# Eight lower parts of a weight stream by accumulating transfers, decay rows through DRAM, and small products at other places

## The chip, the cores and the metric

The kernel runs on one core of one Trainium2 chip, as one program. The metric is device time in microseconds (us). PE is the tensor engine, DVE the vector engine, ACT the scalar (activation) engine, POOL the general engine, SP the sync engine, whose queue issues most DMA loads. The time before is 1096.87 us, the median of 3 runs (1096.74 to 1097.33).

## The reference

A two-layer model on 256 tokens of width 1024, in float32. Each layer has three residual sub-layers, each with its own adaptive norm (`modulate`): a SwiGLU block, a mixer, a SwiGLU block. The mixer of the first layer is the hybrid, in which this change lies; that of the second is an mLSTM.

```python
def hybrid_mixer(h, w_in, w_out, ...):
    gate_lru, x_lru, z_ssd, xbc, dt_raw = jnp.split(h @ w_in, HYB_SPLITS, axis=-1)
    x_lru = causal_conv(x_lru, lru_conv_w, lru_conv_b)
    y_lru = rg_lru(x_lru, ...) * jax.nn.gelu(gate_lru)
    xbc = jax.nn.silu(causal_conv(xbc, ssd_conv_w, ssd_conv_b))
    ...
    dt = jax.nn.softplus(dt_raw + ssd_dt_bias)
    a = -jnp.exp(ssd_a_log)
    y = ssd_chunked(xs, dt, a, bm, cm) + ssd_d[:, None] * xs
    y = y.reshape(bsz, seq, SSD_WIDTH) * jax.nn.silu(z_ssd)
    y = rms_norm(y in 2 groups of 512, ssd_norm_g)
    return jnp.concatenate([y_lru, y], axis=-1) @ w_out
```

`ssd_chunked` works on two chunks of 128 tokens and 16 heads of 64. With `acs` the running sum of `dt * a` within a chunk, a head's weights between tokens are `exp(acs[t] - acs[s])` for s <= t, times the products of `C` and `B`; what the first chunk leaves for the second is weighted with `exp(acs[t])`. So every head needs its row `acs[t]` on all 128 partitions: the decay rows.

## The kernel before

**Weights.** All weights form one stream of 128x128 tiles in the order of use, in pieces of 8 tiles (128 x 1024 floats, 512 KB). `Weights._piece` loads a piece on SP's queue (`wraw`, 4 buffers), ACT writes its high part (`whi`, line 101, the value rounded to the format of the fast products), DVE the lower part, raw minus high (`wlo`, line 102). High and low buffers have three tags, taken in turn by `i % 3`, with two buffers each, so a piece takes the buffers of the piece six before it. `multiply` makes three products of each tile: high weight with high and with low activations, low weight with high activations (lines 443 to 445). A piece is 24 products. The stage of the hybrid starts at piece 66 (`starts[1]`) and has 54 pieces.

**Order.** A planner orders the instructions of each engine by the program's order and its own costs. Where that isn't wanted, the kernel adds edges: `W.behind(i, n, ins)` puts the high (n = 0) or low (n = 1) part of piece i behind an instruction; `stand(m, s, n)` puts a small product behind the n-th weight product of stage s; `in_one_go` keeps products together. `pump` starts the blocks of the adaptive norm (`ada`, 512 KB and one DVE operation over 128 x 1024 each) at the pieces of `ADA_PLAN`, behind the last lower part (`W.last`).

**The hybrid's order on PE.** `begin` makes the first four blocks (`bc`), then two blocks of `xbc`, the dt product, six more blocks of `xbc`, then a loop over c = 0..9 with the block `xl` of c and, two steps behind it, the blocks `z` and `ri` (LRU gates). In this loop stand the small products of the SSD part: `acs` (running sums, at c = 3), their transposition `acst` (at c = 4), the values and states of both groups. Then a loop over four pairs of blocks (m0 = 0, 2, 4, 6; four heads each): decay rows, `y` products, two gate blocks `gl`, and for m0 = 2 and 6 the group's norm. Then the projection out (`od`).

**The parts that the change touches.**
- dt: `dt_weights` keeps high and low parts of the dt weights in two tiles (`wdh`, `wdl`), and three products per k (lines 818 to 820) make 24.
- Decay rows: `decay_rows` writes the transposed sums as high and low part into `stk` (lines 864 and 865). For each pair four products with a selecting vector `sel` spread the rows over the partitions into PSUM (`ab`, line 974). ACT takes them from there: eight `Relu` with the bias `acs` (line 983), two `Exp` for `ce` (985), one `Exp` over all (986). DVE multiplies with `cb` and `C` (988, 992), then PE makes the 24 records of `y` (1008).
- Group norm: `rs_tokens` sums the squares of a group with four products, from the two halves of `gacc` (8 records of `rst_g`, line 359). Eight small DVE operations make the root (`rsy_g`, line 329), `spread` brings it to all partitions (`rsb_g`, line 405).
- The five scans of the LRU that stand around the second group's root are on line 1057.

## Time and profile before

| | |
|---|---|
| runs | 1096.74, 1096.87, 1097.33 us |
| profiled execution | 1097.25 us, its span 1095.5 us |
| busy, share of the span | PE 99%, weight loads 98%, DVE 84%, ACT 58%, POOL 1% |
| granted clock of PE | 0.999 of full speed |
| DMA | 272.34 MB, mean 249 GB/s |
| hybrid stage, first to last PE product | about 194 to 367 us |

Busy shares are means over the whole span; the stage in question is read by itself, in stretches. A PE product is shown from its start to its modelled end, and products overlap: the distance from start to start is what each costs. A row of a timeline has start, length, engine, line, operation, output and inputs, how many were merged, and in brackets the idle time ahead of it with what ended it. "Idle" there is shorter than the hole in the row of products, since the product before it is still running.

### The profile page before, as it was taken

The numbers are of one execution on the slowest core, as the hardware profiler recorded it, in microseconds if no ns is written. First come the engines' busy times: TensorE is split into PE (matmuls) and PEld (weight loads), VectorE is DVE, ScalarE is ACT, GpSimd is POOL, SyncE is SP. The second block draws the span as 40 slices with busy tenths as digits, with TensorE's granted clock in tenths as the row PEclk, the third lists the DMA queues.
The fourth block names the chain that finished last, engine by engine and source line by source line (L and its number), as shares of the span: only waits on it lengthen the run. The fifth ranks groups of instructions, "written<-read, shape, count | busy, mean of one in ns | idle before, by whom it ended". The sixth has DMA issues, their size and how long they took to land.

```text
span 1095.5 us, 23272 instructions
## 1 busy us (share of the span) xinstructions
PE 1083.8 (99%) x9315; PEld 1070.4 (98%) x9315; DVE 920.5 (84%) x1654; ACT 639.5 (58%) x1053; POOL 8.8 (1%) x28
## 2 busy tenths in 40 slices
PE   9999999999999999999999999999999999999997
PEld 7999999999999999999999999999999999999997
DVE  7999999899999899989698798979768868866552
ACT  5765555678986564554454455448776655544452
POOL 0000000000000000000000000010000000000000
PEclk9999999999999999999999999999999999999999
DMA  9889999556855489999848799963432664875551
GB/s 375 344 318 391 387 352 343 178 196 195 279 167 191 139 307 370 354 351 327 281 142 323 266 356 346 338 204 119 146 102 81 208 193 137 298 239 193 193 174 39
DMA packets 75534, 272.34 MB, mean 249 GB/s; under 512 B 8593, under 2 KB 9393, under 8 KB 75426
## 3 DMA queue, kind: packets, MB, share of 16 engines
q1 hardware_dynamic: 74592, 269.38, 69.7%
q8 instruction: 73, 1.20, 0.4%
q0 software_dynamic: 400, 1.04, 0.4%
q10 hardware_dynamic: 434, 0.43, 0.1%
q14 instruction: 35, 0.29, 0.1%
HBM read 269.77 MB, written 1.05 MB: 247 GB/s over the span
## 4 chain that ended last, share of the span: by engine, by line
PE 80%; DVE 12%; DMA 4%; issue 2%; ACT 1%; ACTq 0%; DVEq 0%; SPq 0%
PE gu L445 12%; PE gu L444 12%; PE gu L443 11%; PE od L445 10%; PE od L443 10%; PE od L444 10%; DVE wlo L102 4%; DMA wraw<-in_wst_dram 3%; PE zz L445 1%; PE zz L443 1%; PE zz L444 1%; DMA wgr<-in_ml_wg_dram 1%; DVE ada L262 1%; DVE xc L733 1%; PE gu_f L509 1%
## 5 line engine op out<-in xcount | busy, mean ns | idle before, releaser
L102 DVE TENSOR_TENSOR wlo<-wraw,whi 128x1024 fp32r<-128x1024 f32 x364 | 442.9, 1221 | 83.6 <-ACT whi L101 83.0
L101 ACT CAST whi<-wraw 128x1024 fp32r<-128x1024 f32 x364 | 378.2, 1050 | 210.9 <-DMA wraw<-in_wst_dram 80.2
L444 PE MATMUL gu<-hb,whi 128*128 128x256 f32 x1296 | 358.0, 276 | 0.4 <-DVE hb L668 0.3
L443 PE MATMUL gu<-hb,whi 128*128 128x256 f32 x1296 | 358.0, 276 | 0.0
L445 PE MATMUL gu<-hb,wlo 128*128 128x256 f32 x1296 | 357.9, 276 | 0.1
L444 PEld LDWEIGHTS gu<-hb,whi 128*128 128x128 f32 x1296 | 243.3, 188 | 0.8 <-DVE hb L668 0.8
L445 PEld LDWEIGHTS gu<-hb,wlo 128*128 128x128 f32 x1296 | 243.3, 188 | 0.2 <-DVE wlo L102 0.2
L443 PEld LDWEIGHTS gu<-hb,whi 128*128 128x128 f32 x1296 | 243.2, 188 | 0.0
L443 PE MATMUL od<-ph,whi 128*128 128x256 f32 x704 | 194.3, 276 | 0.0
L444 PE MATMUL od<-ph,whi 128*128 128x256 f32 x704 | 194.3, 276 | 0.0
L445 PE MATMUL od<-ph,wlo 128*128 128x256 f32 x704 | 194.3, 276 | 0.0
L262 DVE SCALAR_TENSOR_TENSOR ada<-ada,cact 128x1024 f32<-128x1024 f32 x144 | 175.3, 1218 | 1.4 <-DMA ada<-in_adaT_dram 1.3
L444 PEld LDWEIGHTS od<-ph,whi 128*128 128x128 f32 x704 | 132.1, 188 | 0.0
L445 PEld LDWEIGHTS od<-ph,wlo 128*128 128x128 f32 x704 | 132.1, 188 | 0.0
L443 PEld LDWEIGHTS od<-ph,whi 128*128 128x128 f32 x704 | 132.1, 188 | 0.0
L426 ACT CAST ph<-fg 128x256 fp32r<-128x256 f32 x88 | 35.1, 406 | 114.9 <-DVE fg L595 114.9
L427 DVE TENSOR_TENSOR ph<-fg,ph 128x256 fp32r<-128x256 f32 x88 | 36.4, 421 | 14.2 <-ACT ph L426 14.2
L416 ACT ACTIVATE sq_o<-x 128x256 f32<-128x256 f32 x42 | 17.5, 418 | 45.6 <-DVE x L571 40.6
L571 DVE SCALAR_TENSOR_TENSOR x<-od,gate,x 128x256 f32<-128x256 f32 x48 | 23.1, 481 | 24.4 <-PE od L445 24.2
L444 PE MATMUL zz<-hb,whi 128*128 128x256 f32 x128 | 36.2, 283 | 0.0
L445 PE MATMUL zz<-hb,wlo 128*128 128x256 f32 x128 | 36.1, 282 | 0.0
L443 PE MATMUL zz<-hb,whi 128*128 128x256 f32 x128 | 35.8, 279 | 0.0
(431 smaller groups left out, 1959.1 us busy)
## 6 DMA issues: line engine op xcount, KB each, us to landing
wraw<-in_wst_dram SPq DMA_DIRECT2D x366, 512.0 KB, 4.6
ada<-in_adaT_dram SPq DMA_DIRECT2D x144, 512.0 KB, 5.6
xn<-in_x_dram SPq DMA_DIRECT2D x2, 512.0 KB, 4.0
wgr<-in_ml_wg_dram POOLq DMA_DIRECT2D x3, 256.0 KB, 5.4
out_dram<-res SPq DMA_DIRECT2D x3, 128.0 KB, 2.4
out_dram<-res ACTq DMA_DIRECT2D x1, 256.0 KB
out_dram<-res SPq DMA_DIRECT2D x1, 256.0 KB, 2.9
cols<-in_cols_dram SPq DMA_DIRECT2D x1, 190.0 KB, 9.5
```

The source lines that it names most:

```text
L101: raw_hi = nc.scalar.copy(hi, raw)
L102: self.last = nc.vector.tensor_tensor(out=lo, in0=raw, in1=hi.bitcast(F32), op=ALU.subtract)
L262: return nc.vector.scalar_tensor_tensor(out=raw, in0=raw, scalar=1.0, in1=cact, op0=ALU.mult, op1=ALU.mult, accum_out=mods[s][:, m:m + 1])
L416: square = nc.scalar.activation(q, x, AF.Square).ins
L426: nc.scalar.copy(hi, src)
L427: nc.vector.tensor_tensor(out=both[:, 1, :], in0=src, in1=hi.bitcast(F32), op=ALU.subtract)
L443: m = nc.tensor.matmul(dst, wh, both[:, 0, :], start=start, stop=False, skip_group_check=True)
L444: W.products += [m, nc.tensor.matmul(dst, wh, both[:, 1, :], start=False, stop=False, skip_group_check=True), nc.tensor.matmul(dst, wl, bo ...
L445: nc.tensor.matmul(dst, wl, both[:, 0, :], start=False, stop=stop, skip_group_check=True)]
L509: W.products += [nc.tensor.matmul(dst, wh, rh, start=(k == 0), stop=False), nc.tensor.matmul(dst, wh, rl, start=False, stop=False), nc.ten ...
L571: nc.vector.scalar_tensor_tensor(out=xs_t[d], in0=dst, scalar=g[:, d:d + 1], in1=xs_t[d], op0=ALU.mult, op1=ALU.add)
L733: nc.vector.scalar_tensor_tensor(out=dst[:, o:], in0=src[:, :T - o], scalar=cw(j), in1=dst[:, o:], op0=ALU.mult, op1=ALU.add)
```

## The change

1. **Lower parts by accumulating transfers.** For the pieces 76, 79, 82, 85, 88, 91, 94 and 106 the lower part isn't made on DVE. ACT writes the negated value, rounded, into `wlo`, and a DMA on POOL's queue adds the piece from DRAM to it a second time. `W.last` stays at the last lower part made on DVE.
2. **Decay rows.** ACT copies the transposed sums into `rows`, SP stores them in DRAM (`kept`, 16 x 256), and `decay_tile` loads the rows of a pair's four heads on all partitions (`mt`, 512 KB, SP). The spreading products, `stk` and `sel` go. `decay_pair` then works in SBUF: one `Exp` for `ce` of both blocks, eight `Relu` and one `Exp` in place. The first two pairs' tiles are loaded at c = 5 and 7 and worked on at c = 7 and 9 of the loop before; those of the other two are loaded behind the `y` products of m0 = 0 and 2, whose buffers they take.
3. **Fewer products.** The dt weights lie with high and low side by side in one tile, so 16 products give both, and DVE adds the two results. DVE adds the two halves of `gacc` (`folded`) before the group's sum.
4. **Places.** `y` of m0 = 0 and 2 behind products 732 and 795 of the stage, the second group's sum behind 934 and its spread behind 995. The lower parts of the pieces 75 and 97 behind conv sums, of 105 and 109 behind the groups' roots. The scans behind the second root. The eight ada blocks of this stage over its pieces 22 to 34 rather than 37. The first group's outputs are split right behind its norm, within the loop over the pairs.

```diff
-SUMS = {"n1": (1, 11), "n2": (2, 11), "n4": (4, 14)}
+SUMS = {"n1": (1, 11), "n2": (2, 11), "n4": (4, 14), "g1": (1, 934)}
+SPREADS = {"n2": (2, 28), "g1": (1, 995)}
+ADDED = (76, 79, 82, 85, 88, 91, 94, 106)
...
-    (0, (17, 43), range(16, 40)), (0, (43, 65), range(48, 64)), (1, (22, 37), range(40, 48)),
+    (0, (17, 43), range(16, 40)), (0, (43, 65), range(48, 64)), (1, (22, 34), range(40, 48)),
...
             raw_hi = nc.scalar.copy(hi, raw)
-            self.last = nc.vector.tensor_tensor(out=lo, in0=raw, in1=hi.bitcast(F32), op=ALU.subtract)
...
+            if added:
+                low = nc.scalar.activation(lo, raw, AF.Copy, scale=-1.0)
+                nc.gpsimd.dma_start(lo, self.src[i].bitcast(F32R), accum_op=ALU.add)
+            else:
+                low = nc.vector.tensor_tensor(out=lo, in0=raw, in1=hi.bitcast(F32), op=ALU.subtract)
...
+                if i == 0:
+                    W.behind(starts[1] + 9, 1, taps[-1])
...
-            nc.tensor.matmul(b[:, 0:T], wdh, h[k][:, 0, :], start=(k == 0), stop=False)
-            nc.tensor.matmul(b[:, 0:T], wdh, h[k][:, 1, :], start=False, stop=False)
-            nc.tensor.matmul(b[:, 0:T], wdl, h[k][:, 0, :], start=False, stop=(k == ND - 1))
+            for i in range(2):
+                nc.tensor.matmul(b[:, 0:T], dt_parts[:, 32 * k:32 * k + P], h[k][:, i, :], start=(k == i == 0),
+                                 stop=(k == ND - 1 and i == 1))
...
+        nc.vector.tensor_tensor(out=dt, in0=both[:, :, 16:32], in1=dt, op=ALU.add)
...
-            nc.vector.tensor_copy(stk[0:16, :], b[0:16, 0:T])
-            nc.vector.tensor_tensor(out=stk[32:48, :], in0=b[0:16, 0:T], in1=stk[0:16, :].bitcast(F32),
-                                    op=ALU.subtract)
+            nc.scalar.copy(rows[0:16, :], b[0:16, 0:T])
+            nc.sync.dma_start(kept, rows[0:16, :])
+
+        def decay_tile(m0):
+            mt = wk.tile([P, 2, 2, 2, P], F32, tag="mt", name=f"mt{m0}", bufs=2)
+            nc.sync.dma_start(mt.rearrange("p n i c t -> p (n i c t)"),
+                                kept.rearrange("(q h) t -> q (h t)", q=4)[m0 // 2:m0 // 2 + 1].to_broadcast([P, 4 * T]))
+            decays[m0] = mt
...
+        def decay_pair(m0):
+            g = m0 // 4
+            mt = decays.pop(m0)
+            ce = wk.tile([P, 2, 2, P], F32, tag="ce", name=f"ce{m0}", bufs=2)
+            expo = nc.scalar.activation(ce.rearrange("p n i t -> p (n i) t"),
+                                        mt.rearrange("p n i c t -> p (n i) c t")[:, :, 1, :], AF.Exp)
+            for n in range(2):
+                for i in range(2):
+                    for c in range(2):
+                        hd = 2 * (m0 + n) + i
+                        nc.scalar.activation(mt[:, n, i, c, :], mt[:, n, i, c, :], AF.Relu,
+                                             bias=acs[:, c, hd:hd + 1], scale=-1.0)
+            nc.scalar.activation(mt, mt, AF.Exp, scale=-1.0)
...
+            return mt, ce, needed, expo
...
+                if c == 7:
+                    W.behind(starts[1] + 31, 1, taps[-1])
...
+            if c in (5, 7):
+                decay_tile(c - 5)
+            if c in (7, 9):
+                pairs[c - 7] = decay_pair(c - 7)
...
-            ab = [ax_bank(f"ab{m}") for m in pair]
...
-                    nc.tensor.matmul(b[:, i * T:(i + 1) * T], sel[:, hd:hd + 1].to_broadcast([P, P]), stk,
-                                     start=True, stop=True)
...
+            mt, ce, needed, expo = pairs.pop(m0) if m0 in pairs else decay_pair(m0)
...
+            if m0 < 4:
+                stand(products[0], 1, (732, 795)[m0 // 2])
...
+                folded = nc.vector.tensor_tensor(out=gacc[:, 0, :], in0=gacc[:, 0, :], in1=gacc[:, 1, :], op=ALU.add)
+            if m0 < 4:
+                decay_tile(m0 + 4)
...
-                roots.append(rs_tokens([gacc[:, 0, :], gacc[:, 1, :]], 512, f"g{g}", "q"))
+                roots.append(rs_tokens([gacc[:, 0, :]], 512, f"g{g}", "q"))
...
+                W.behind(starts[1] + (39, 43)[g], 1, rsqrt_ends[-1])
...
+                with tc.issue_after(second_root.ins):
+                    nc.vector.tensor_tensor_scan(out=xl[:, c, :], data0=av[:, c, :], data1=nq[:, c, :], initial=0.0,
+                                                 op0=ALU.mult, op1=ALU.add)
```

More of the change, by code (lines that the diff above doesn't have):

```diff
@@ L88, in __init__ @@
         self.splits = {}
+        self.last = None
         self.after = {}
@@ L99, in _piece @@
         hi, lo = (self.part_pool.tile([P, w], F32R, tag=f"{n}{'abc'[i % 3]}", name=f"{n}{i}") for n in ("whi", "wlo"))
+        added = i in ADDED
         with self.tc.high_priority(offset=self.ahead):
             raw_hi = nc.scalar.copy(hi, raw)
-            self.last = nc.vector.tensor_tensor(out=lo, in0=raw, in1=hi.bitcast(F32), op=ALU.subtract)
-        if i < 2:
-            self.tc.add_manual_dep(self.last.ins, self.first.ins.name, NOSYNC, reason="the first input first")
-        self.parts[i] = (hi, lo)
-        self.splits[i] = (raw_hi, self.last)
-        if i - 1 in self.splits:
-            for n in range(2):
-                self.tc.add_manual_dep(self.splits[i][n].ins, self.splits[i - 1][n].ins.name, NOSYNC, reason="in order")
+            if added:
[3 more added lines that the diff above has]
+                low = nc.vector.tensor_tensor(out=lo, in0=raw, in1=hi.bitcast(F32), op=ALU.subtract)
+        self.parts[i] = (hi, lo)
+        if self.splits:
+            self.tc.add_manual_dep(raw_hi.ins, self.splits[max(self.splits)][0].ins.name, NOSYNC, reason="in order")
+        if added:
+            self.splits[i] = (raw_hi, self.last)
+            return
+        if self.last is not None:
+            self.tc.add_manual_dep(low.ins, self.last.ins.name, NOSYNC, reason="in order")
+        self.last = low
+        self.splits[i] = (raw_hi, low)
         for n, ins in self.after.pop(i, ()):
@@ L144, in body @@
     partp = ctx.enter_context(tc.tile_pool(name="partp", bufs=2))
+    dramp = ctx.enter_context(tc.tile_pool(name="dramp", bufs=1, space=bass.MemoryType.DRAM))
     at = FIRST_PLACE
@@ L754, in exp_neg_abs @@
         return e, nc.scalar.activation(e, e, AF.Exp).ins
-    dt_parts = [cst.tile([P, 8 * 16 + 112], F32R, name=n) for n in ("wdh", "wdl")]
+    dt_parts = cst.tile([P, 480], F32R, name="wd")
     def dt_weights():
@@ L847, in hybrid @@
         acs = acs_wide[:, 0:32].rearrange("p (c h) -> p c h", c=2)
-        stk = sp.tile([P, T], F32R, name="stk")
-        nc.gpsimd.memset(stk.bitcast(F32), 0.0)
+        rows = sp.tile([P, T], F32, name="rows")
+        kept = dramp.tile([16, T], F32, name="kept")
         dec = sp.tile([P, 16], F32, name="dec")
@@ L872, in hybrid @@
         o = COL["lru_ba"]
-        sel = sp.tile([P, 16], F32R, name="sel")
+        sp.tile([P, 16], F32R, name="pad3")
         with tc.issue_after(W.normed.ins):
             nc.vector.tensor_scalar(out=hb, in0=cols[:, o:o + 16], scalar1=0.5, scalar2=None, op0=ALU.mult)
-            nc.vector.tensor_tensor(out=sel, in0=ident[:, 0:16], in1=ident[:, 32:48], op=ALU.add)
         b = ax_bank("bn", "p")
@@ L1028, in hybrid @@
             if m0 % 4 == 2:
-                roots.append(rs_tokens([gacc[:, 0, :], gacc[:, 1, :]], 512, f"g{g}", "q"))
+                roots.append(rs_tokens([gacc[:, 0, :]], 512, f"g{g}", "q"))
                 if g == 0:
                     group_norm(0)
-        ys = [sp.tile([P, 2, T], F32R, tag=f"ssd{m % 4}{m // 4}", name=f"ysb{m}") for m in range(8)]
-        for m in range(4):
-            split(xs[:, m, :], ys[m])
+                W.behind(starts[1] + (39, 43)[g], 1, rsqrt_ends[-1])
+                ys += [sp.tile([P, 2, T], F32R, tag=f"ssd{m}{g}", name=f"ysb{4 * g + m}") for m in range(4)]
+                if g == 0:
+                    for m in range(4):
+                        split(xs[:, m, :], ys[m])
+        second_root = rsqrt_ends[-1]
         yl, last = [], []
```

57 lines of the change are left out of this document (22 added, 35 removed).

## The prediction

> **What bounds the kernel now.** I read the page first (engine shares, the chain that ended last), then the waits of PE in the hybrid stage, then a table of stretches, then PE's order of time around each wait. From the page:
>
> ```profile
> PE 1083.8 (99%) x9315; PEld 1070.4 (98%) x9315; DVE 920.5 (84%) x1654; ACT 639.5 (58%) x1053; POOL 8.8 (1%) x28
> PE 80%; DVE 12%; DMA 4%; issue 2%; ACT 1%; ACTq 0%; DVEq 0%; SPq 0%
> ```
>
> PE is the bound: only fewer products or fewer holes between them shorten this kernel. The 12% of DVE in the chain say where the holes come from. The waits of PE between 212 and 332 us (total, times, longest):
>
> ```profile
> PE y L1008 <- DVE mt L988: 0.8, 1, 0.8
> PE z L443 <- DVE lru_x L733: 0.8, 1, 0.8
> PE rsb_g L405 <- DVE rsy_g L329: 0.7, 1, 0.7
> PE xbc L443 <- DVE ssd_x L733: 0.3, 1, 0.3
> ```
>
> Each is a wait for DVE. The stretches (busy us of PE, PEld, DVE, ACT, POOL, granted clock, DMA share, GB/s) say why:
>
> ```profile
> 220.00:250.00 30.00, 29.73 (x262) 29.56 (x261) 28.75 (x67) 23.07 (x42) 0.00 (x0) 1.00 0.57 186
> 250.00:283.00 33.00, 33.00 (x281) 31.96 (x279) 32.68 (x60) 26.90 (x52) 0.00 (x0) 1.00 0.67 222
> 283.00:296.00 13.00, 11.71 (x98) 11.18 (x96) 13.00 (x24) 12.74 (x31) 0.00 (x0) 1.00 0.89 297
> 296.00:332.00 36.00, 34.79 (x336) 33.32 (x337) 34.97 (x69) 31.68 (x64) 0.00 (x0) 1.00 0.51 167
> ```
>
> From 220 to 296 us DVE has 28.75 + 32.68 + 13.00 = 74.4 of 76 us of work, ACT 62.7. Both are near full here, at a granted clock of 1.00, so the stage has two engines a few per cent behind PE. The holes in order of time on PE (start, length, operation, idle before):
>
> ```profile
> 220.24 0.28 PE L445 MATMUL xbc<-hb,wlo 128*128 128x256 f32 x1
> 220.79 0.36 PE L443 MATMUL xbc<-hb,whi 128*128 128x256 f32 x1 [0.28 <-DVE ssd_x L733]
> ...
> 282.85 0.28 PE L445 MATMUL ri<-xlb,wlo 128*128 128x256 f32 x1
> 283.90 0.39 PE L443 MATMUL z<-hb,whi 128*128 128x256 f32 x1 [0.77 <-DVE lru_x L733]
> ...
> 295.28 0.28 PE L443 MATMUL gl<-hb,whi 128*128 128x256 f32 x1
> 296.41 0.33 PE L1008 MATMUL y<-mt,ssd 128*64 128x128 f32 x2 [0.85 <-DVE mt L988]
> ...
> 330.61 0.28 PE L445 MATMUL od<-ysb,wlo 128*128 128x256 f32 x1
> 331.61 0.46 PE L405 MATMUL rsb_g<-ident,rsy_g 128*128 128x128 f32 x2 [0.72 <-DVE rsy_g L329]
> ```
>
> A product takes 0.28 us, but the next starts 0.12 us after it (below). So a hole costs its start-to-start distance less 0.12: 0.43, 0.93, 1.01 and 0.88, together 3.25 us.
>
> **The change, part by part.**
>
> *Fewer dt products.* 24 products become 16. The first of them and the first product after them:
>
> ```profile
> 212.08 0.28 PE L818 MATMUL dtT<-hb,wdh 128*128 128x256 f32 x1
> ...
> 214.89 0.28 PE L443 MATMUL xbc<-hb,whi 128*128 128x256 f32 x1
> ```
>
> 2.81 us / 24 = 0.117 us each; 8 fewer are -0.94 us, all on PE. The added DVE sum over 128x32 elements costs PE nothing: DVE has it early, in a stage where its load falls (below).
>
> *Decay rows through DRAM, and fewer sum products.* From the chain in order of time, one pair's products, four spreads of decay rows and the eight sums of one group:
>
> ```profile
> 301.58 1.46 PE y L1008 x24
> 304.19 0.47 PE ab L974 x4
> 308.22 0.87 PE rst_g L359 x8
> ```
>
> The 16 `ab` products go: 16 x 0.117 = -1.87. Of the 16 records of `rst_g` eight go, because the two halves are added on DVE first: 8 x 0.109 = -0.87. In their place come one fold per group on DVE (256 elements per partition, about 0.4 us, a third of the lower part's 1.22 below) and DMAs on SP: one store and four 512 KB loads. PE work together: -0.94 - 1.87 - 0.87 = **-3.7 us**.
>
> *What queues behind the new DMAs.* SP issues in order. The tile loads for the third and fourth pair wait until PE has done with the buffers, and the weight loads behind them wait too. The high cast of the weight piece whose load comes next behind the third pair's tile load, and PE's first product with it:
>
> ```profile
> 288.15 1.04 ACT L101 CAST whi<-wraw 128x1024 fp32r<-128x1024 f32 x1
> ...
> 307.26 0.28 PE L443 MATMUL gl<-hb,whi 128*128 128x256 f32 x1
> ```
>
> There are 19 us between them. The loads (KB, median us to landing):
>
> ```profile
> wraw<-in_wst_dram SPq DMA_DIRECT2D x366, 512.0 KB, 4.6
> ```
>
> So this piece's load was issued by 283.5. Behind the tile load it waits for the end of `y0`, whose products start 46 products earlier than before: 296.41 less the hole of 1.01, less 46 x 0.115 = 5.3, less 0.47 for the `ab` products that stood between, is 289.6, and 291.1 with the 1.46 they take. Of the 19 us some 11 remain: nothing. If this cover were gone it would cost up to 7.6.
>
> *Eight lower parts.* One lower part on DVE, and two high casts on ACT:
>
> ```profile
> L102 DVE TENSOR_TENSOR wlo<-wraw,whi 128x1024 fp32r<-128x1024 f32 x364 | 442.9, 1221 | 83.6 <-ACT whi L101 83.0
> 217.54 2.01 ACT L101 CAST whi<-wraw 128x1024 fp32r<-128x1024 f32 x2
> ```
>
> DVE loses 8 x 1.22 = 9.8 us, ACT gains 8 x 1.0 = 8 us (the negated copy, same size as the cast), POOL gains eight issues. Seven of the eight lie between 217 and 283 us. DVE there: 74.4 - 7 x 1.22 = 65.9; two ada products that come earlier (1.2 each by size) and the second pair's multiplication (the 1.22 of the same size plus half) bring it to 70 of the some 73 us that the stretch then lasts. So three of the four holes, which are DVE lateness, lose their reason. ACT: 62.7 + 7 + 0.4 for the row copy, and the second pair's exponentials may come in from behind 296. Their first and last row, eleven instructions:
>
> ```profile
> 295.52 1.24 ACT L983 ACTIVATE mt<-ab,acs 128x128 f32<-128x128 f32 x4
> ...
> 298.09 1.19 ACT L986 ACTIVATE mt<-mt 128x1024 f32<-128x1024 f32 x1
> ```
>
> 3.8 us: ACT then has 73.9 in a stretch of 73. That is the price of this change, and I return to it.
>
> *The transfer's latency.* The trace has no accumulating transfer. The nearest rows besides that of the weight loads (a load by POOL; then the weight loads' min/median/max):
>
> ```profile
> wgr<-in_ml_wg_dram POOLq DMA_DIRECT2D x3, 256.0 KB, 5.4
> DMA to landing us min/median/max: 3.3/4.6/9.7
> ```
>
> Lower bound 3.3, the quickest load of this size. Upper bound 2 x 9.7 = 19.4: it reads both source and destination. I take 6.5, between the POOL row, which is the nearest in queue, and twice the SP median. Who waits: PE, for the lower part of that piece. The first such piece is the earliest and tightest. Its high cast starts at 217.54 (above); PE's first product of it:
>
> ```profile
> 226.33 0.28 PE L443 MATMUL xbc<-hb,whi 128*128 128x256 f32 x1
> ```
>
> After: 217.5 + 1.0 (cast) + 1.0 (copy) + 6.5 = 226.0. PE gets there 0.94 + 0.43 earlier, at 225.0: late by 1.0 us; since the cast may be issued a little sooner I take +0.7 (0 at 5.5 us or less, 13.9 at 19.4). A later one, the fifth:
>
> ```profile
> 248.63 1.04 ACT L101 CAST whi<-wraw 128x1024 fp32r<-128x1024 f32 x1
> ...
> 262.83 0.28 PE L443 MATMUL z<-hb,whi 128*128 128x256 f32 x1
> ```
>
> 14.2 us, less 2.0 and less 1.5 by which PE is earlier: 10.7 for the transfer. It is hidden at 6.5.
>
> The Trainium skill ("DMA: Bandwidth & Descriptors", section Anatomy of one DMA) fits a transfer from GpSimd as about 2.0 us plus bytes over 436 GB/s, an estimate of 3.2 us for 512 KB; by that the first piece is not late and the sum is 0.7 lower. The row of 4.6 us for the same size under this kernel's load disagrees with the fit already. The skill ("SBUF — State Buffer", section Summary: rules for kernel authors) also advises against a software-generated DMA under a busy DVE, since its descriptors starve while DVE runs in its two-port modes; by its section Who interferes with whom a two-input operation such as the lower part only takes a read port. By the advice alone the first piece would wait for one such operation more, by the other nothing; I add nothing.
>
> *Small products at other places.* Rows of DVE that made the holes: two lower parts ahead of the conv sums that `xbc` waits for; and the second group's root, from its first row to its last, with a scan before nearly each of its steps:
>
> ```profile
> 216.33 2.36 DVE L102 TENSOR_TENSOR wlo<-wraw,whi 128x1024 fp32r<-128x1024 f32 x2
> ...
> 324.43 0.16 DVE L373 TENSOR_SCALAR rsv_g<-rst_g 128x2 f32<-128x2 f32 x1
> ...
> 330.73 0.69 DVE L1057 TENSOR_TENSOR_SCAN lru_x<-lru_aq 128x256 f32<-128x256 f32 x1
> 331.33 0.14 DVE L329 SCALAR_TENSOR_TENSOR rsy_g<-rsw_g,rsy_g 128x2 f32<-128x2 f32 x1
> ```
>
> The root took 7 us for nine small steps; with the scans and a lower part behind it, it ends by about 326, and its spread is due at product 995 of the stage (it stood at 987), near 332: the last hole goes, -0.88. One of the two lower parts goes behind the conv sums: 1.2 us against a hole of 0.43, but PE comes 0.94 earlier for the dt products saved. Bounds -0.43 and +0.2; I take -0.3. The hole at 283 goes with DVE's load, -0.93. `y0` moves ahead from product 778 to 732, to 289.6 by the times of before (above). Its multiplications released PE at 296.41, so they have to come 7 us earlier. The rows they start from stood ready here before:
>
> ```profile
> 260.64 0.40 DVE L864 CAST stk<-acst 16x256 fp32r<-16x256 f32 x1
> ```
>
> From 260.6 the store and the tile load take two transfers, 9 us by the median above and 19 by the longest, then 4 us of exponentials and 2 of multiplications: 276 to 286, against 289.6 less the 2.8 that PE is then ahead, 286.8. It fits, without room at the upper end. If it does, the hole of 1.01 goes. Sum of the holes: -0.88 - 0.3 - 0.93 - 1.01 = **-3.1 us**. What is late next is ACT with its 73.9 in 73 us; I put +0.6 on it (0 if the second pair's exponentials stay behind 296, 3.1 if it brings all the holes back).
>
> *The sum.* -3.7 - 3.1 + 0.7 + 0.6 = **-5.5 us**. The profiled execution took 1097.25 us, 1.75 more than its span, 0.38 over the median of the runs: 1097.25 - 5.5 - 0.38 = **1091.4 us**. Before 212 and after 332 us I change nothing: PE is full there, so the end moves by what the stage gains.
>
> **The rivals.**
>
> 1. *ACT becomes the bound* (the waits change their engine). For it: 73.9 us of work in 73, its row of 12.74 in 13, `y0` due earlier. Against it: its high casts run 9 to 19 us ahead of PE and can give way. PE's work falls by 3.7, the holes stay as ACT's: 1096.87 - 3.7 = 1093.2, between 1092.5 and 1094.7.
> 2. *Slower: the accumulating transfers land too late.* Only PE waits for them, at the first piece. With every other gain kept (-3.7 - 3.1 + 0.6 = -6.2) it decides from a latency where the delay is 6.2: 5.5 + 6.2 = 11.7 us. At twice the longest load, 19.4, the first piece costs 13.9; the fifth one's 10.7 grows by the delay already taken and holds. Time 1096.87 - 6.2 + 13.9 = 1104.6; half way, at 15 us, 1100.2. For it: two reads for a write, a DMA share of 0.89 where the later pieces lie. Against it: 0.57 where the first lies, and POOL's median of 5.4.
> 3. *The change does nothing for the holes and the work saved turns into waits* (PE comes to each conv, root and pair earlier by what it saved, and DVE has only 3 us to spare in 73): 1096.9. Against it: the casts run 9 to 19 us ahead, so of 8.5 us less DVE work more than the 0.94 and 0.43 is left for the late operations.
> 4. *All of it works*: no late first piece and no ACT bound, 1096.87 - 3.7 - 3.25 = 1089.9, and down to 1088.8 if re-entries of PE after the removed insertions save 0.1 us each at some ten places.
>
> **How the numbers follow.** Forecast (1090.5 to 1092.5) 0.40; rival 4 (1088.8 to 1090.5) 0.20; rival 1 (1092.5 to 1094.7) 0.22; rival 3 (1094.7 to 1099.1) 0.06; rival 2 (above) 0.12. A measurement here tells 0.2% from nothing, 2.2 us: faster is 0.40 + 0.20 + 0.22 = 0.82, same 0.06, slower 0.12. The range leaves out rival 2 and the upper part of rival 3, 0.12 and some 0.04, and a little below rival 4: 1088.8 to 1096.0. The forecast's own range is 1090.5 to 1092.5.
>
> **What would show it.** Right: 16 `dtT` products and no `ab` on PE, eight `rst_g` records; no wait of PE for `lru_x`, `mt` or `rsy_g` between 212 and 332 us; the stretch from the stage's first dt product to the spread of the second group shorter by 5 to 6 us; DVE below full from 220 to 290. The transfers: their rows from issue to landing give the latency, 6.5 us or not; a PE wait at a lower part `wlo` for a DMA would show rival 2, and its length the price. ACT rows without a gap and PE waits for ACT would show rival 1. The prediction is wrong if new waits of PE add up to more than 3 us, or if the gain lies outside this stage.

## The result, and the profile after

Measured: **1108.4 us** (median of 4 runs, 1103.73 to 1111.23) against 1096.88 us before, a ratio of 1.0100 with a 95% interval of 1.0065 to 1.0135. The change makes the kernel slower; 1091.4 us was predicted. The profiled execution took 1107.94 us, its span is 1105.8 us.

From the page of the changed kernel, the busy times and the chain that ended last:

```profile
PE 1086.2 (98%) x9283; PEld 1071.5 (97%) x9283; DVE 913.1 (83%) x1646; ACT 647.0 (59%) x1058; POOL 15.3 (1%) x34
PE 82%; DVE 8%; DMA 5%; issue 3%; ACT 3%; ACTq 0%; DVEq 0%; SPq 0%; POOLq 0%
```

PE has 32 records fewer and is busy 2.4 us longer, so some products ran slower. In the chain DVE fell from 12% to 8%; DMA and ACT took its place. The waits of PE between 212 and 385 us (total, times, longest):

```profile
PE xbc L457 <- DMA wlo<-in_wst_dram: 3.9, 1, 3.9
PE ri L455 <- ACT lru_aq L941: 2.3, 1, 2.3
PE od L455 <- ACT ysb L438: 1.1, 1, 1.1
PE rst_n L371 <- ACT sq_o L428: 1.0, 1, 1.0
PE y L1035 <- issue: 0.8, 2, 0.5
PE gl L455 <- ACT thi L943: 0.8, 1, 0.8
PE od L456 <- DVE ysb L439: 0.3, 1, 0.3
```

The four waits for DVE of before are gone, as predicted. New and longer ones stand in their place: for a transfer, for ACT, and one at the sum of the next stage.

**The first transfer.** Piece 76 in order of time, on ACT, on POOL and on PE:

```profile
217.91 1.06 ACT L105 CAST whi<-wraw 128x1024 fp32r<-128x1024 f32 x1
218.87 1.06 ACT L107 ACTIVATE wlo<-wraw 128x1024 fp32r<-128x1024 f32 x1
...
220.24 0.89 POOL L108 DMA_DIRECT2D wlo<-in_wst_dram  x1 [27.51 <-PE xbc L457]
...
225.69 0.28 PE L456 MATMUL xbc<-hb,whi 128*128 128x256 f32 x1
229.82 0.58 PE L457 MATMUL xbc<-hb,wlo 128*128 128x256 f32 x1 [3.86 <-DMA wlo<-in_wst_dram]
230.20 0.41 PE L455 MATMUL xbc<-hb,whi 128*128 128x256 f32 x1
230.41 0.41 PE L456 MATMUL xbc<-hb,whi 128*128 128x256 f32 x1
```

Cast and copy come as predicted. The transfer takes 9.6 us from issue to landing, and PE waits. Behind the wait a product starts 0.21 us after the one before, not 0.115. The stretches around it (busy PE, PEld, DVE, ACT, POOL, granted clock, DMA share, GB/s) say why:

```profile
220.00:225.90 5.90, 5.89 (x50) 5.76 (x50) 5.90 (x10) 4.50 (x8) 0.89 (x1) 1.00 0.87 215
225.90:229.80 3.90, 0.06 (x1) 0.00 (x0) 0.57 (x2) 1.60 (x3) 0.88 (x1) 0.88 0.96 313
229.80:235.70 5.90, 5.88 (x27) 5.88 (x28) 4.31 (x7) 3.75 (x6) 0.00 (x0) 0.50 0.99 266
235.70:250.00 14.30, 14.30 (x128) 14.30 (x127) 11.14 (x35) 11.96 (x22) 1.71 (x2) 1.00 0.83 235
```

The granted clock is 0.50 right behind the hole, for 27 products. The Trainium skill describes this ("TensorE: Matmul & The Clock Gate", section What's actually happening): after an idle window of about 3.4 us PE runs at half rate, and the windows run freely. The trace agrees: the half clock lasted 6.83 us, two times 3.41.

**The decay rows.** The tile loads on SP's queue, and the operation of ACT that waits for the first:

```profile
265.22 0.34 SPq L881 DMA_DIRECT2D kept<-rows  x1
...
276.03 0.38 SPq L885 DMA_DIRECT2D mt<-kept  x1
...
285.84 0.63 ACT L958 ACTIVATE ce<-mt 128x512 f32<-128x512 f32 x1 [3.54 <-DMA mt<-kept]
```

Behind this 3.54 us ACT's own gates come late, and PE waits 2.3 and 0.8 us for them. The transfers (KB, median us from issue to landing; the last line is the shortest, median and longest of `wlo`):

```profile
wlo<-in_wst_dram POOLq DMA_DIRECT2D x8, 512.0 KB, 9.1
mt<-kept SPq DMA_DIRECT2D x4, 512.0 KB, 8.3
kept<-rows SPq DMA_DIRECT2D x1, 16.0 KB, 6.6
...
DMA to landing us min/median/max: 7.2/9.1/10.4
```

**Where the time went.** How late PE is against the kernel before at the first product of a piece, less what it was already at piece 68, before the edits (us, worked out from the starts of the products in both traces; piece 120 is the first of the next stage, 260 lies in a later one). Each row is one profiled execution; those without the transfer at 76 and with transfers at 110 and 111 only are the fastest of their runs:

| kernel | 76 | 77 | 94 | 99 | 107 | 112 | 120 | 122 | 260 |
|---|---|---|---|---|---|---|---|---|---|
| changed | -1.1 | 5.3 | 5.8 | 6.0 | 5.9 | 7.0 | 7.0 | 9.6 | 10.2 |
| no transfer at 76 | -1.2 | -1.2 | -0.1 | 0.0 | -0.1 | 0.9 | 0.9 | 3.1 | 3.1 |
| transfers that write, not add | -1.2 | -0.4 | 0.7 | 1.4 | 0.8 | 1.8 | 1.8 | 4.1 | 5.1 |
| no transfer at all | -1.2 | -1.2 | -0.9 | -3.4 | -3.9 | -2.9 | -2.9 | 0.8 | 0.5 |
| eight lower parts left out | -1.2 | -1.2 | -1.1 | -4.2 | -4.4 | -3.3 | -3.3 | -0.5 | 0.1 |
| no transfer, scans free | -1.1 | -1.1 | -1.1 | -4.1 | -4.6 | -0.2 | -0.2 | -0.2 | -0.5 |
| four left out behind the root | -1.2 | -1.2 | -1.2 | -3.8 | -4.3 | -3.3 | -3.3 | -3.3 | -3.5 |
| transfers 110, 111 only | -1.1 | -1.1 | -1.0 | -4.4 | -5.2 | -3.1 | -3.1 | -2.6 | -2.9 |
| before, eight transfers alone | 0.0 | 4.3 | 4.3 | 3.9 | 4.3 | 8.2 | 8.2 | 8.3 | 8.0 |
| before, fewer products alone | -0.1 | -0.1 | -0.3 | -0.5 | 2.9 | 1.6 | 1.6 | 1.6 | 1.7 |

The experiments below explain its rows. The theories: A, the first transfer and the half clock behind it; B, ACT overloaded by the copies; C, the tile of decay rows; D and later E, DVE sets the pace. "Without transfers" is the second experiment's kernel.

### The profile page after: what moved, and what is told of

Its sections match the earlier page's. It is cut to its first block, busy times and chain, and to the rows that moved or that the text cites. A ratio compares the mean times of both kernels' runs of the same rounds, so it can differ in the third digit from the quotient of the medians.

```text
span 1105.8 us, 23225 instructions
## 1 busy us (share of the span) xinstructions
PE 1086.2 (98%) x9283; PEld 1071.5 (97%) x9283; DVE 913.1 (83%) x1646; ACT 647.0 (59%) x1058; POOL 15.3 (1%) x34
## 4 chain that ended last, share of the span: by engine, by line
PE 82%; DVE 8%; DMA 5%; issue 3%; ACT 3%; ACTq 0%; DVEq 0%; SPq 0%; POOLq 0%
PE gu L456 12%; PE gu L457 12%; PE gu L455 12%; PE od L456 8%; PE od L455 8%; PE od L457 8%; DVE wlo L110 3%; DMA wraw<-in_wst_dram 2%; PE zz L455 1%; PE zz L457 1%; PE zz L456 1%; PE gu_f L523 1%; PE gu_f L521 1%; PE gu_f L522 1%; DMA mt<-kept 1%
## 5 line engine op out<-in xcount | busy, mean ns | idle before, releaser
L110 DVE TENSOR_TENSOR wlo<-wraw,whi 128x1024 fp32r<-128x1024 f32 x356 | 433.0, 1220 | 91.4 <-ACT whi L105 89.6
```

Source lines behind the costliest of these rows:

```text
L110: low = nc.vector.tensor_tensor(out=lo, in0=raw, in1=hi.bitcast(F32), op=ALU.subtract)
```

## The experiments

**1. No transfer at 76.**

```diff
-ADDED = (76, 79, 82, 85, 88, 91, 94, 106)
+ADDED = (79, 82, 85, 88, 91, 94, 106)
```

> The changed kernel, but the lower part of piece 76 is made on DVE again; the other seven stay accumulating transfers. Theory A (the first accumulating transfer is late: it took 9.6 us from issue to landing, PE waited 3.9 us for it, and behind this hole PE's granted clock was 0.5 for 6.83 us, which cost another 2.6 to 2.9 us): 1108.4 - 4.0 - 2.7 = 1101.7 us, no wait of PE for a DMA near 226 us and no stretch of half clock at 229 to 236; the wait of ACT for the tile of decay rows (3.5 us) and the holes behind 282 us stay. Rival B (ACT has too much work with eight more copies, and the wait at 76 only takes up lateness that would come anyway): 1107 or more, with the loss back as other waits of PE before 283 us.

Measured 1103.86 us (ratio to before 1.0065, 1.0041 to 1.0088). No wait at 76 and no half clock at 229 to 236; in the table the end moves from 10.2 to 3.1. A holds: the two profiles differ by 6.5 us at piece 77 and by 7.1 at the end. Between the medians it is 4.5 us; this profile (1100.27 us, with no half clock) is the fastest of five runs that go up to 1108.66. But it isn't all: between the pieces 77 and 99 PE loses 1.2 us, and it waits 1.0 us for the transfer of piece 94.

**2. No transfer at all.**

```diff
-ADDED = (76, 79, 82, 85, 88, 91, 94, 106)
+ADDED = ()
```

> The changed kernel with all eight lower parts on DVE again; decay rows through DRAM, fewer products and the new places stay. Theory A (only the first of the eight transfers is late, the other seven are hidden): no better than without 76 alone, 1101 to 1104 us, as DVE gets 8.5 us of work back. Theory C (the tile of decay rows, 9.8 us from issue to landing, holds ACT, and so the holes of 2.6 and 1.06 us at 288 and 295 us come): these holes are there unchanged. Rival B (the eight copies overload ACT): the holes at 288 and 295 us go, 1097 to 1099 us.

Measured 1098.61 us (1.0009, 1.0000 to 1.0019). Better than theory A expected: my claim that the other seven are hidden is refuted. It is the time that B gave, so B has to be judged by its cause. Without them PE is 3.4 us earlier at piece 99. The stretch from 226 to 283 us, first without the transfer at 76, then without any (columns as above):

```profile
226.00:283.00 57.00, 55.42 (x473) 53.90 (x472) 48.62 (x110) 48.84 (x92) 5.19 (x6) 1.00 0.92 271
```

```profile
226.00:283.00 57.00, 57.00 (x491) 55.84 (x490) 55.46 (x118) 47.07 (x94) 0.00 (x0) 1.00 0.70 228
```

The transfers take DVE from 55.5 to 48.6 us and leave ACT at 48.8 of 57: neither is full, so B's overload isn't there. What is nearly full is the DMA share, 0.92 against 0.70. And the other transfers become slower. Without any transfer:

```profile
mt<-kept SPq DMA_DIRECT2D x4, 512.0 KB, 6.5
kept<-rows SPq DMA_DIRECT2D x1, 16.0 KB, 3.4
```

6.5 and 3.4 us in place of 8.3 and 6.6 (7.3 and 7.4 without the transfer at 76). No run has the copies on ACT without the transfers, so it is argued and not shown that the traffic, and not the copies' place in ACT's order, makes the loss.

**3. The kernel before with the eight transfers alone.** The class `Weights` and `ADDED` of the changed kernel, nothing else.

> The kernel before with the eight accumulating transfers alone; none of the other edits. Theory A: PE waits 3.5 to 4.5 us at piece 76 and its clock falls to a half behind it, +6 to +7 us there; with DVE 9.8 us lighter up to 2 us of its holes go: 1101 to 1104 us. Rival B: no hole at 76 of that size, but ACT's lateness through the stage. If the transfers are harmless without the rest: 1095 to 1097 us.

Measured 1105.29 us (1.0071, 1.0057 to 1.0085), outside the range by 1.3 us. The hole at 76 and one window of half clock cost 4.3 us (piece 77); the hole at 283 us for DVE goes. The other 4 us are lost between the pieces 107 and 112: PE waits 1.4 us for the second group's outputs, and a second window of half clock follows.

**4. The kernel before with fewer products alone.** 16 dt products, one folded half per group.

> The kernel before with only the two edits that take products from PE: 16 dt products in place of 24, and group sums from one folded half (8 records fewer). Theory: PE is the bound, so it is 8 x 0.117 + 8 x 0.109 = 1.8 us faster, 1095.1 us. Rival: DVE's lateness takes the saved time back as waits, 1096.9 us.

Measured 1099.39 us (1.0011, 1.0001 to 1.0021): 1.8 us less PE work, and not faster. Its waits of PE in this stage:

```profile
PE rsb_g L405 <- DVE rsy_g L329: 1.4, 1, 1.4
PE z L443 <- DVE lru_x L733: 1.2, 1, 1.2
PE od L444 <- DVE ysb L427: 0.9, 1, 0.9
PE xbc L443 <- DVE ssd_x L733: 0.8, 1, 0.8
PE y L1008 <- DVE mt L988: 0.5, 1, 0.5
```

The waits for DVE add up to 4.8 us; in the four rows of before it was 2.6. DVE took back what PE saved. Each fold is also a step of DVE ahead of its group's sum, so this run shows PE's saving together with the folds.

**5. Transfers that write in place of adding.**

```diff
-                nc.gpsimd.dma_start(lo, self.src[i].bitcast(F32R), accum_op=ALU.add)
+                nc.gpsimd.dma_start(lo, self.src[i].bitcast(F32R))
```

> The changed kernel, whose eight transfers on POOL's queue write the piece into the buffer instead of adding it (so the lower part is left out: these eight pieces are multiplied with the raw weights in its place). Same bytes written, same queue, same order of all instructions. If the adding is what makes the transfer long: issue to landing falls from 7.2/9.1/10.4 us (shortest, median, longest) to about 5 to 6 us, and the wait of PE at piece 76 from 3.9 us to at most 0.5, with no half clock behind it. If the queue of POOL or the load on the DMA engines is what makes it long: 8 us or more, and the wait stays.

One run, 1103.66 us. The transfers of `wlo`, and PE's wait at 76:

```profile
wlo<-in_wst_dram POOLq DMA_DIRECT2D x8, 512.0 KB, 6.0
...
DMA to landing us min/median/max: 4.6/6.0/7.1
...
PE xbc L457 <- DMA wlo<-in_wst_dram: 0.4, 1, 0.4
```

So the adding costs 3.1 us a transfer (9.1 against 6.0). What keeps 6.0 above the 4.7 of the weight loads in this run isn't taken apart. The predicted 6.5 us was right for a transfer that only writes. Yet with such transfers the kernel is still slower than before: ACT waits 2.0 us for the first tile of decay rows, PE 2.2 us for ACT's gates with a window of half clock behind it, and 2.1 us at the sum of the next stage. A right latency alone would not have made the forecast right.

**6. A hole made by DVE in the kernel before.**

```diff
+    tc.add_manual_dep(W.products[3 * PIECE * 125 + 2].ins, W.splits[128][1].ins.name,
+                      mybir.DependencyInfo(mybir.DependencyClass.Sync, mybir.DependencyReason.DATA), reason="a hole")
+    for k in range(3 * PIECE * 125 + 2, 3 * PIECE * 127):
+        tc.add_manual_dep(W.products[k + 1].ins, W.products[k].ins.name, NOSYNC, reason="in order")
```

> The kernel before, in whose third stage the first low product of piece 125 waits for the lower part of piece 128 (DVE), and the products behind it keep their order. No transfer is changed, and PE's order of products is that of before. By the times of before the lower part ends at 387.8 us and the product was due at 383.1: a hole of 4.6 us. Theory A (a hole of some 4 us takes the granted clock to 0.5 behind it): products 0.21 us apart in place of 0.115 for one or two stretches of 3.41 us, so 1.6 to 3.3 us more than the hole: 1096.9 + 4.6 + 1.6 to 3.3 = 1103 to 1105 us. Rival (the slow products after piece 76 came from the transfers and loads in memory, not from the hole): 1101.5 us, with products 0.115 us apart right behind the hole.

Measured 1104.36 us (1.0056, 1.0041 to 1.0071). PE around the hole, and two stretches behind it:

```profile
383.17 0.28 PE L444 MATMUL gu<-hb,whi 128*128 128x256 f32 x1
387.91 0.38 PE L445 MATMUL gu<-hb,wlo 128*128 128x256 f32 x1 [4.46 <-DVE wlo L102]
```

```profile
388.76:392.18 3.42, 3.42 (x19) 3.42 (x18) 3.18 (x4) 0.36 (x2) 0.00 (x0) 0.50 0.80 225
392.18:400.00 7.82, 7.82 (x70) 7.82 (x70) 6.51 (x10) 4.02 (x6) 0.00 (x0) 1.00 0.91 316
```

A hole of 4.74 us from start to start, 4.6 over a product's distance, costs 6.4: the rest is one window of half clock. This kernel has no accumulating transfer, and behind the window products run at full clock with a higher DMA share (0.91), so the slow products are the clock's, not memory's.

**7. Tiles of decay rows from another source**, on the kernel of experiment 1.

```diff
-            nc.sync.dma_start(mt.rearrange("p n i c t -> p (n i c t)"),
-                                kept.rearrange("(q h) t -> q (h t)", q=4)[m0 // 2:m0 // 2 + 1].to_broadcast([P, 4 * T]))
+            nc.sync.dma_start(mt.rearrange("p n i c t -> p (n i c t)"), a["adaT"][m0])
```

> The changed kernel without the transfer at 76, whose four tiles of decay rows are loaded from another array in DRAM, each partition its own 4 KB (the decay weights are left out of the result: other numbers stand in their place). The load no longer waits for the store of the rows, and no 128 partitions read the same 4 KB. If the shared source makes the tile load long: from 8.3 us (median, issue to landing) to the 4.8 us of a weight load, and the wait of ACT for the first tile (2.3 us without the transfer at 76) is gone, and PE's holes for ACT at 281 to 289 us (1.3, 1.0 and 0.9 us over a product's distance) shrink. If the load on the queue makes it long: 7 us or more, and the wait stays at 1 to 2.3 us.

One run, 1107.15 us. The loads took 8.3 us, against 7.3 in the kernel of experiment 1 (medians of four loads), and ACT waited 4.3 us for the first, against 2.3. So neither the shared 4 KB nor the store makes them long. With experiment 2 the traffic beside them is what remains: without the eight transfers the same loads take 6.5 us.

**8 and 9. Other places, with few transfers.** Eight: transfers at 106 and 108, the first pair one step later, other stands. Nine: transfers at 106, 107 and 108, and the first group's sum at 862.

```diff
-SUMS = {"n1": (1, 11), "n2": (2, 11), "n4": (4, 14), "g1": (1, 934)}
+SUMS = {"n1": (1, 11), "n2": (2, 11), "n4": (4, 14), "g0": (1, 862), "g1": (1, 934)}
-ADDED = (76, 79, 82, 85, 88, 91, 94, 106)
+ADDED = (106, 107, 108)
```

> The changed kernel with accumulating transfers only at 106 and 108 (their casts run 14 to 18 us ahead of PE, against some 11 us that a copy and a transfer take); the first pair's exponentials one step later (c = 8), its products at 755 and the second pair's at 800; the first group's sum at 862, the second group's spread at 985, and the two wide multiplications ahead of the scans behind the second root. Against the kernel without transfers (1098.6 us) it should lose the wait of ACT for the tile (2.1 us), the hole at the first group's sum (1.4), those at the second group's outputs (1.2) and with DVE 2.4 us lighter most of the one at the next stage's sum (2.1, and 1.7 of half clock): 1092 to 1096 us. If DVE and ACT are full through the stage whatever the places are, the holes come back elsewhere: 1097 to 1099 us.

> The changed kernel with accumulating transfers only for 106, 107 and 108, whose casts end 13.6 to 17.9 us ahead of PE, and the first group's sum 14 products later (862). Against 1098.6 us without any transfer: the hole at that sum goes (1.4 us), DVE is 3.7 us lighter from 318 us on, so the holes behind the second spread (1.2 us) and at the next stage's sum (2.1 us) shrink: 1093 to 1096 us. If the transfers (8.5 us from issue to landing) land late or only the places count: 1097 to 1099 us.

Measured 1101.38 us (1.0044, 1.0018 to 1.0070) and 1098.26 us (1.0009, 1.0000 to 1.0017). In the profile of the first (1106.72 us, of runs from 1098.45 to 1110.88) PE waits 3.0 us for the second group's folded sum and 2.4 at the next stage's sum, with two windows of half clock behind each. In the second no transfer is late, PE is 4.1 us ahead at piece 107, and still loses it: 2.0 us at the sum of the next stage. Lighter by 3.7 us, DVE only waits longer for PE's group sums (1.9 us in place of 0.7). This led to the next two.

**10. Eight lower parts left out.** `lo = hi` for the eight pieces, with neither copy nor transfer.

> The changed kernel with neither the transfer nor the copy nor the DVE operation for the eight pieces: their lower part is left out of the computation, and the third product of each tile takes the high part again. So DVE has 9.8 us less work than in the kernel without transfers (1098.6 us), at no cost to ACT and the queues; everything else is as there. Theory D (in this stage DVE sets the pace: the 3.7 us less PE work were taken back as waits for DVE's late results): 1091 to 1094 us. Rival (the places, and the tile of decay rows that ACT waits for, set it): 1097 us or more, with the waits for ACT at 281 to 289 us, at the second group's outputs and at the sum of the next stage (2.1 us) unchanged.

Measured 1097.49 us (1.0000, 0.9991 to 1.0008). D falls in this form: 9.8 us less on DVE brings no more than 1.1 us between the medians. In the table all is well up to piece 107; then the gain goes at the same two places.

**11. Scans not held behind the root**, on the kernel without transfers.

```diff
-                with tc.issue_after(second_root.ins):
-                    nc.vector.tensor_tensor_scan(out=xl[:, c, :], data0=av[:, c, :], data1=nq[:, c, :], initial=0.0,
-                                                 op0=ALU.mult, op1=ALU.add)
+                nc.vector.tensor_tensor_scan(out=xl[:, c, :], data0=av[:, c, :], data1=nq[:, c, :], initial=0.0,
+                                             op0=ALU.mult, op1=ALU.add)
```

> The kernel without transfers (1098.6 us), its scans no longer held behind the second group's root. Theory: the hold moves some 3 us of scans on DVE behind the root, DVE's last residual sum of the stage comes that much later, and so PE waits 2.0 us at the sums of the next stage, with half clock behind; without the hold this wait falls below 0.5 us, and the root and its spread come 2 to 3 us later, which PE pays there: 1097 to 1099 us, the hole moved from 366 to 328 us. Rival: the wait at the next stage's sum stays at 2 us, as DVE is behind for another reason.

Measured 1097.49 us (1.0005, 0.9996 to 1.0014). As expected the hole moves: none at the next stage's sum, and at the second group

```profile
PE rsb_g L417 <- DVE rsy_g L341: 1.7, 1, 1.7
...
PE od L455 <- ACT ysb L438: 1.2, 1, 1.2
```

Between the pieces 107 and 112 it loses 4.4 us. In both places of the scans the 4 us go.

**12. Four lower parts left out behind the root** (110 to 113, as in 10).

> The changed kernel without transfers, in which the lower parts of the pieces 110 to 113 are left out of the computation (the third product takes the high part again): 4.9 us less on DVE, all of it behind the second group's root. Theory E (from the second group's root at some 323 us to the last residual sum at 366 us DVE has no gap, so what PE gains before is lost as the wait at the next stage's sum; work taken from DVE ahead of the root, as in the run with eight lower parts left out, cannot help): the wait there (2.0 us) falls below 0.4 us and no half clock follows it: 1098.6 - 2.7 - 0.9 = 1095 us, less than with eight lower parts left out ahead of it (1097.5). Rival (that wait is ACT's, or one of the order of DVE's last operations): it stays at 2 us, 1098 us.

Measured **1094.97 us** (0.9975, 0.9965 to 0.9985): half the work left out, at another place, and faster than before. The wait at the next stage's sum is gone; without transfers it was

```profile
PE rst_n L371 <- ACT sq_o L428: 2.0, 1, 2.0
```

where ACT squares what DVE has just summed.

The stretch from the second group's root to the last residual sum, without transfers and here:

```profile
324.90:367.70 42.80, 40.27 (x346) 39.50 (x346) 41.31 (x72) 28.13 (x43) 1.06 (x2) 1.00 0.61 200
```

```profile
324.90:365.00 40.10, 38.99 (x338) 38.43 (x337) 36.31 (x66) 27.46 (x43) 0.71 (x2) 1.00 0.63 208
```

E holds. In the first row DVE has 41.3 us of work in 42.8 and PE 40.3: behind the root DVE is the bound. The root hangs on PE's sum of the second group, and this sum came no earlier than before. The root's first row on DVE, in the kernel before and in the one without transfers:

```profile
324.43 0.16 DVE L373 TENSOR_SCALAR rsv_g<-rst_g 128x2 f32<-128x2 f32 x1
```

```profile
324.91 0.16 DVE L385 TENSOR_SCALAR rsv_g<-rst_g 128x2 f32<-128x2 f32 x1 [0.74 <-PE rst_g L371]
```

By the order of PE's products in the traces, the sum stood behind product 931 of the stage before and behind 965 here: the 934 of the edit is only the earliest place. These 34 products are 3.9 us, the whole lead that PE had at piece 107. With eight lower parts left out (experiment 10) the sum stood behind 951; the root started 2.0 us earlier than without transfers (322.92 against 324.91 us) and the next stage's sum 1.2 us earlier. So work taken from DVE ahead of the root counts only as far as it lets the sum stand earlier.

Order has a part in DVE's lateness too. Without transfers DVE makes the lower part of piece 123 (1.22 us) at 362.78 us, ahead of its last residual sums, though PE's first product of that piece starts at 378.59. No run puts it behind them.

**13. Ways to keep that gain.** Transfers for 111 and 112; four transfers with an earlier second sum and spread; the residual's sums of squares on POOL; these and the scans' gate products on POOL; transfers for 110 and 111. All on the kernel without transfers.

```diff
+            eng = nc.gpsimd if nm.startswith("o1_") else nc.vector
+            eng.tensor_tensor(out=acc[0], in0=acc[0], in1=q, op=ALU.add)
```

> The changed kernel with accumulating transfers for 111 and 112 alone, whose lower parts DVE makes behind the second group's root. Theory E: DVE is 2.4 us lighter where it has no gap, the wait at the next stage's sum shrinks from 2.0 us to at most 0.5; the transfers have 13.0 and 12.8 us from the cast to PE and need 10 to 11: 1095 to 1097 us. Rival (the transfers land late, or ACT's copies delay the second group's outputs): 1098 us or more.

> The changed kernel with accumulating transfers for 106, 107, 111 and 112; the first group's sum at 862, the second group's sum 12 products earlier (922) and its spread at 983. By theory E both count, the root that starts 1.2 us earlier and the 2.4 us that DVE is lighter behind it: 1093 to 1096 us. If the fold isn't ready for the earlier sum, PE waits there by up to 1.4 us: 1097 us.

> The changed kernel without any accumulating transfer, whose six running sums of squares of this stage's residual (0.33 us each on DVE, issued from 355 to 367 us) are made on POOL instead, which is idle there. By theory E (no gap on DVE behind the second group's root) that is 2.0 us less on DVE in the place that counts: the wait at the next stage's sum falls from 2.0 us to about 0.3 and no half clock follows: 1098.6 - 1.7 - 0.9 = 1096.0 us, 1095 at best. POOL's price for a sum of 128x256 isn't in any trace so far; it may be up to 2.3 us each without harm, as they stand 2.3 us apart. If POOL takes longer, or slows DVE beside it, the wait stays: 1098 us or more.

> The same, and two edits more: the four products of the scans with the gate (128x512, 0.60 us each on DVE) on POOL too, and the first group's sum 14 products later (862). By theory E another 2.4 us off DVE behind the root and 0.7 us less hole at the first group's sum: 1094 to 1095.5 us. If POOL needs more than some 2 us for one, the outputs of the LRU part come late and PE waits for them: 1098 us or more.

> The changed kernel with accumulating transfers for 110 and 111 alone: both copies stand on ACT ahead of its table load at 328.8 us, so the transfers are issued at about 327.3 and 329.3 us and, at 9.4 us, land at 336.7 and 338.7 us, 1.2 and 1.8 us ahead of PE. Theory E: 2.4 us less on DVE behind the root and no late transfer: the wait at the next stage's sum falls from 2.0 us to at most 1.0, 1095.5 to 1097 us. If the copies (2 us) delay ACT's casts and the second group's outputs instead, or a transfer takes over 10.6 us: 1098 us or more.

Measured: 1099.47 us (1.0011, 1.0000 to 1.0021), 1103.48 (1.0047, 1.0033 to 1.0060), 1101.20 (1.0027, 1.0017 to 1.0038), 1104.32 (1.0058, 1.0044 to 1.0072) and 1096.65 (0.9996, 0.9987 to 1.0005). The first fails by the transfer of 112, whose copy stands behind a table load on ACT: PE waits 2.2 us for it. The second fails where its rival said, with 2.9 us of wait for the fold in place of the 1.4 given. In the third and fourth PE waits 3.2 and 4.5 us at the next stage's sum. On POOL a sum takes 1.0 us, and DVE is slower beside it. Between 355 and 367 us (busy, mean ns), first without transfers, then with POOL's sums:

```profile
L502 DVE SCALAR_TENSOR_TENSOR hb<-x,scale,hb 128x256 fp32r<-128x256 f32 x6 | 2.9, 482 | 0.0
```

```profile
L503 DVE SCALAR_TENSOR_TENSOR hb<-x,scale,hb 128x256 fp32r<-128x256 f32 x6 | 5.4, 907 | 0.6 <-ACT hb L502 0.6
...
L433 POOL TENSOR_TENSOR ssq<-ssq,sq_o 128x256 f32<-128x256 f32 x6 | 6.0, 998 | 168.7 <-ACT sq_o L428 168.6
```

DVE loses 6 x 0.425 = 2.6 us and saves the 2.0 of the expectation. The Trainium skill has the rule ("SBUF — State Buffer", section Who interferes with whom): a DVE instruction with two inputs in SBUF contends with a GpSimd instruction that reads SBUF. This row agrees.

Transfers at 110 and 111, the last, keep most of the gain in the profile (-2.9 at piece 260), but this profile, 1094.46 us, is the fastest of its runs: ten took up to 1098.77 us, one 2812.66. Over its runs it is level with before. It is the best that leaves nothing out, 1% faster than the changed kernel, and no measurable gain over the one before.

**14. The kernel before with three transfers that have room** (85, 88, 106).

> The kernel before with three accumulating transfers alone, at 85, 88 and 106, whose high casts ran 12.9, 13.4 and 17.2 us ahead of PE in the profile of before, so that a copy of 1 us and a transfer of 9.1 us fit. Theory A: no wait for a transfer and no half clock; DVE is 2.4 us lighter before 283 us, and the holes for DVE at 283 and 296 us (0.93 and 1.01 us) shrink: 1095.5 to 1097 us. Rival (any accumulating transfer costs, through ACT or through the loads beside it): 1098.5 us or more.

Measured 1101.96 us (1.0042, 1.0030 to 1.0055): the rival. No wait for a transfer, no half clock, and still PE loses 3.7 us from piece 94 to 112, at

```profile
PE od L455 <- ACT ysb L438: 1.4, 1, 1.4
PE y L1020 <- DVE mt L1000: 1.2, 1, 1.2
PE z L455 <- DVE lru_x L745: 1.1, 1, 1.1
```

The first is one of order: here DVE has two scans and a lower part between the root and the outputs (335.5 to 337.8 us), before it had a lower part alone (331.4 to 332.5). With three pieces off DVE the planner, which orders each engine by its costs, set the scans otherwise. Whether order or traffic makes the other two stays open.

## Why the prediction was wrong, point by point

- **The transfer's latency.** This step failed first. 6.5 us was taken; the eight took 7.2 to 10.4, median 9.1, and the first 9.6. What was missing is the adding, 3.1 us (experiment 5): the value was put by rows of transfers that only write. The bounds, 3.3 to 19.4, held. PE was delayed by 4.0 us in place of 0.7. The fit of the Trainium skill ("DMA: Bandwidth & Descriptors", section Anatomy of one DMA), 3.2 us, disagrees with both medians, 6.0 and 9.1. With 6.0 us PE waited 0.4 us here, but one run of that kernel took 1103.66 us: the steps below fail as well.
- **The deciding latency of rival 2.** Its mechanism came true, at a chance of 0.12, but 11.7 us was too high a threshold: the hole was priced at its length. Behind it the clock halved, for 2.9 us more (from -1.1 at piece 76 to 5.8 at 94, less 4.0). No term of the sum held the clock. Experiment 6 shows it without a transfer. The Trainium skill, which I didn't weigh, speaks for it ("TensorE: Matmul & The Clock Gate", section HAM oscillation — how this bites in real kernels).
- **"The fifth is hidden", and nothing for the rest.** Wrong. With the first removed, the other seven cost 3.4 us by piece 99: one was late by 1.0 us at 94, and beside them (DMA share 0.92 against 0.70) a store took 7.4 us for 3.4 and the tile loads 7.3 for 6.5. How much of the rest is their traffic and how much their copies on ACT stays open.
- **The decay rows, "fits, without room at the upper end".** Without transfers this held: no wait of PE for `mt`. Two things were left out. SP, in order, issued the load well behind the store (10.8 us, of which the store takes 6.6), and the operation that waits for the tile stands in ACT's order ahead of the gates that PE needs: 2.1 us of ACT without transfers, 3.5 with them, and then 2.3 and 0.8 us of PE.
- **ACT, 73.9 us in 73.** Wrong in size: 60.8 us in the 74 from 226 to 300 us. The 62.7 of 76 that it started from is 82%, not near full. Rival 1 didn't come by load. Where PE waited for ACT, ACT had waited for a transfer or for its order.
- **PE work, -3.7.** The products went, as counted. Alone, 1.8 us of it brought nothing (experiment 4): rival 3's mechanism, put at 0.06.
- **The holes, -3.1.** All four waits for DVE went; without transfers a new one came, 1.2 us at the first group's folded sum. Up to piece 107 the kernel without transfers is 3.9 to 5.2 us ahead in its variants, not far from the 5.3 that the steps up to there give (0.94 + 1.87 + 0.87 + 0.3 + 0.93 + 1.01 - 0.6). The last step, a root that ends by about 326 us, failed: the sum ahead of it stood behind product 965, not 934, and the root ended at 328.7.
- **"After 332 us I change nothing: PE is full there."** The step that would have failed even with perfect transfers. PE was full there because DVE, busy 41.4 us of the 44.1 from the second group's root to the next stage's sum, was just not late. Without transfers the root started no earlier (324.91 us, 324.43 before), PE lost 1.0 us of its 3.9 by piece 112, and the sum of the next stage waited 2.0 us with half clock behind it, 3.7 us in all (experiments 10 to 12).

The runs of the changed kernel spread over 7.5 us, with a mean granted clock from 0.996 to 0.993. By freely running windows it depends on the launch how many a hole halves; one is 1.7 us. That explains up to half the spread, and is argued, not shown.

## What to carry to other kernels

Price a hole of PE by its length and by the clock behind it, and an accumulating transfer by a row of its own, with what it adds to the loads beside it. Before adding up gains of the bound engine, go down the stage to the place where another engine starts from that engine's result and has no gap up to the next such place. What is gained ahead counts only if that start itself comes earlier, so look in the trace where it stands; behind it, work has to be taken off the other engine. A few moved places change the order of every engine; judge them one at a time.

## What the runs showed of the hardware

- Adding during a 512 KB transfer: 9.1 us median against 6.0 without, same queue, same places (one run of the latter).
- Half clock for one or two windows of 3.41 us stood behind every hole of 2.6 us or more, and behind some shorter ones: in the changed kernel 1.2 us at 376 us were followed by one window, 2.5 us at 288 us by none, and 2.4 us at the same products in experiment 5 by one. Right behind the 1.2 us stood eight products of one column (0.9 us), so what that hole does alone is open. The Trainium skill ("TensorE: Matmul & The Clock Gate", section What's actually happening) speaks of an idle window of about 3.4 us; here holes of 2.4 and 2.6 us were enough.
- 128 partitions that read the same 4 KB of DRAM load no slower than 128 that read their own: 7.3 and 8.3 us (experiments 1 and 7, medians of four loads, the second of one run).
- A sum on POOL beside DVE nearly doubles a DVE operation with two inputs: 482 to 907 ns.
